# Norm output turned back on TensorE, gate row made in the attention phase, shared output in full-row buffers

## The chip, the cores and the metric

The kernel runs on one core of one Trainium2 chip. The metric is the device time of one execution in microseconds (us). The kernel before takes 3271.61 us, the median of 3 runs (3268.63 to 3282.35). The engines are TensorE (PE, and PEld for its weight loads), VectorE (DVE), ScalarE (ACT), GpSimd (POOL) and SyncE (SP, which only issues DMAs here).

## What is computed

512 tokens of width 1024 go through one block of a first network and two layers of a second one, all in float32. Only the middle of the first block matters here. With `c` the conditioning vector, six rows of width 1024 come from it, among them `g1, sh2, sc2, g2`:

```python
mod = (c_act @ w_ada[l] + b_ada[l])[:, None, :]
sh1, sc1, g1, sh2, sc2, g2 = jnp.split(mod, 6, axis=-1)
...
x = x + g1 * (jnp.concatenate([o_hg, o_nsa], axis=-1) @ w_out[l])
h = rmsnorm(x, norm2_g[l]) * (1.0 + sc2) + sh2
x = x + g2 * moe_ffn(h, router_w[l], router_bias[l], w_exp_gu[l], w_exp_dn[l], w_sh_gu[l], w_sh_dn[l])
```

`moe_ffn` scores 64 experts for every token (a sigmoid of `h @ router_w`), takes the best 8 of the best 4 groups of 8, and adds to the weighted output of those experts the output of one shared expert that sees all tokens. Every expert is a gated product of hidden width 256.

## The kernel before

The program runs in phases: a (first norm and its first projections), b (two mixers, attention and the output projection), c (experts) and d (the second network). Matrix products of float32 data are made of three passes over a split of both operands into a rounded high part and a rest: `mm3` (L158 to L162) issues the passes, and `split` (L164 to L167) makes the parts, the high one by a cast on ACT and the rest by a subtraction on DVE.

**The order of the work.** The text of the program is not the order on an engine. A planner places the instructions of each engine by a model of their times (the kernel is built with `schedule_with_timeline_sim=True`), and `after` (L154) pins a few of them behind others. Each engine then works through its own list in order, so an instruction that waits holds back all behind it. POOL's list holds its DMA issues too, SP's those of the weights.

**Rows of the conditioning.** `b_mods` (L395) is a generator. `tick` advances it between pieces of the attention, so that the big products `c_act @ w_ada` are done a few rows at a time beside it: `mod_acc` (L180) multiplies on DVE and adds on POOL into a tile of 128 partial rows. From that, `mod_cols` (L200, matmuls on L205) makes the sum as 8 columns of 128, and `row_bc` (L897, matmuls on L903, sums on L904) makes it as a full row that stands in all 128 partitions. `g2` is made as columns only, `g1` as a row only, `sh2` and `sc2` (here `B2` and `A2`) in both forms. These rows live in the three `macc` buffers.

**The norm before the experts.** The output projection at the end of phase_b runs in two halves `h` of 256 tokens, and each half ends in a norm: sums of squares on ACT (L593), one scaling on DVE to `h2` (L597), then for each pair `k` of 128-column pieces four transposes on PE (L604), a scale and shift into `t2` (ACT L611, DVE L613) and a split into `self.hh, self.hl`. That is the transposed norm, which the router and the shared expert read. The experts gather rows of tokens instead, so the same norm is made a second time in rows: POOL multiplies `h2` by `A2` (L622), adds `B2` (L623), and writes it to memory as `h2d` (L624).

**From the router to the first expert.** `router(1)` on PE gives the logits, ACT copies them (`lgT`, L618), and phase_c (L1019) transposes them, applies the sigmoid (L1058), and makes the choice of experts by a long row of small DVE instructions. Their end is a list of tokens for the first three experts (`iidx`, L1259), which `gather` (L1200, an indirect DMA of POOL's queue) uses to fetch rows of `h2d` into the `ring` tiles, which POOL has set to zero (L1043). Meanwhile the second half of the shared expert runs (`shared_up`, then `shared_down`, L1002). `shared_down` makes eight pieces of 128 tokens by 512 columns; each is multiplied by `g2` on DVE (L1016) into a tile `sy` with two buffers (tag `ey`) and written to `accd[1]` by POOL's queue (L1017). `g2` as a row is made here from its columns: POOL makes eight diagonal tiles (L1065), PE sums them (L1066), ACT copies the result (L1067).

For the experts after the first three, the kernel orders all 64 by their load: it transposes the choice and the weights, copies them to `sT` (L1144, also tag `ey`), permutes them (L1147), and loops over the experts. In PE's list these permutations stand just before and between the first expert's transposes (L1299).

**The loop over experts.** Expert n loads 3 MB of weights by SP's queue, gathers the rows of expert n + 4, and adds its output to `accd` by an indirect DMA.

Of the kernel before, what the change touches and what calls it, by code (L numbers as in the profile page):

```python
# [8 lines left out]
F32 = mybir.dt.float32  # L9
# [5 lines left out]
AF = mybir.ActivationFunctionType  # L15
OP = mybir.AluOpType
AX = mybir.AxisListType

S = 512
# [122 lines left out]
class Kern:  # L142
# [252 lines left out]
    def b_mods(self):  # L395

        yield from self.mod_sub(0, 0, pool=True)
        for v in self.mod_acc(self.p["w_ada"][0], self.cact, 5 * D, pool=True):
            if v is None:
                yield  # L400
        self.g2c = self.cp.tile([128, 8], F32, name="g2c")
        self.mod_cols(v, self.g2c, self.vec("b_ada", 40, 8), "sc")
        yield
        rows, cols = [], []
        for n in (2, 3, 4):
            for v in self.mod_acc(self.p["w_ada"][0], self.cact, n * D, pool=True):
                if v is None:
                    yield
            rows.append(v)
            if n > 2:  # L410
                t = self.cp.tile([128, 8], F32, name=f"mc{n}")
                self.mod_cols(v, t, self.vec("b_ada", n * 8, 8), "sc")
                cols.append(t)
            self.row_bc(v, n * D, "sc")
            yield
        self.g1, self.B2, self.A2 = rows
        self.B2c, self.A2c = cols
        self.nc.vector.scalar_tensor_tensor(self.A2c, self.A2c, 1.0, self.vec("norm2_g", 0, 8), op0=OP.add, op1=OP.mult)
        gb = self.m4.tile([128, D], F32, name="gb", tag="mraw", bufs=2)
        self.nc.gpsimd.dma_start(gb, self.p["norm2_g"][0:1, :].to_broadcast([128, D]))  # L420
        self.nc.vector.scalar_tensor_tensor(self.A2, self.A2, 1.0, gb, op0=OP.add, op1=OP.mult)
        yield

    def kv_proj(self, win):
# [54 lines left out]
    def phase_b(self):  # L479
# [82 lines left out]
        def router(h):  # L562
            hs = slice(h * 256, (h + 1) * 256)
            for k in range(KT):
                self.mm3(psr[0:64, hs], rwh[:, k], rwl[:, k], self.hh[:, k, hs], self.hl[:, k, hs], k == 0, k == KT - 1)

        for h in range(2):
# [31 lines left out]
            for k in range(0, KT, 2):  # L599
                ps = self.bank("tr")  # L600
                for kk in range(2):
                    for ii in range(2):
                        c0 = (2 * kk + ii) * 128
                        nc.tensor.transpose(ps[:, c0:c0 + 128], h2[:, ii, (k + kk) * 128:(k + kk + 1) * 128], self.ident)  # L604
                t2 = mid.tile([128, 512], F32, name="h2t", tag=("kraw", "pct")[k // 2 % 2], bufs=1)
                for kk in range(2):
                    t = t2[:, kk * 256:(kk + 1) * 256]
                    a, b = self.A2c[:, k + kk:k + kk + 1], self.B2c[:, k + kk:k + kk + 1]
                    pv = ps[:, kk * 256:(kk + 1) * 256]
                    if kk:  # L610
                        nc.scalar.activation(t, pv, AF.Identity, bias=b, scale=a)  # L611
                    else:
                        nc.vector.tensor_scalar(t, pv, a, b, op0=OP.mult, op1=OP.add)  # L613
                    self.split(t, self.hh[:, k + kk, hs], self.hl[:, k + kk, hs])
            if h:
                router(1)
                self.lgT = self.m4.tile([128, S], F32, name="lgT", tag="mraw", bufs=2)[0:64]
                nc.scalar.copy(self.lgT, psr[0:64, :])  # L618

            for ii in range(2):  # L620
                i = 2 * h + ii
                nc.gpsimd.tensor_tensor(h2[:, ii], h2[:, ii], self.A2, OP.mult)  # L622
                nc.gpsimd.tensor_tensor(h2[:, ii], h2[:, ii], self.B2, OP.add)  # L623
                nc.gpsimd.dma_start(self.h2d[i * 128:(i + 1) * 128, :], h2[:, ii])  # L624
        self.dump("x1", self.x1[:])

# [375 lines left out]
    def shared_down(self):  # L1002

        nc, c = self.nc, self.cpool
        for i in range(4):
            nc.gpsimd.dma_start(self.accd[0][i * 128:(i + 1) * 128, :], self.x1[:, i])
        for half in range(2):
            cs = slice(half * 512, (half + 1) * 512)
            dh, dl = self.dn_piece(self.shd, half)
            for i in range(4):  # L1010
                ahl = self.sha[i // 2]
                ps = self.bank("dn")
                for k in range(2):
                    self.mm3(ps, ahl[:, 0, i % 2, k], ahl[:, 1, i % 2, k], dh[:, k], dl[:, k], k == 0, k == 1)
                y = c.tile([128, 512], F32, name="sy", tag="ey", bufs=2)
                nc.vector.tensor_tensor(y, ps, self.g2[:, cs], OP.mult)  # L1016
                nc.gpsimd.dma_start(self.accd[1][i * 128:(i + 1) * 128, cs], y)  # L1017

    def phase_c(self):  # L1019
        nc, p, c = self.nc, self.p, self.cpool  # L1020
# [19 lines left out]
        self.ring = []  # L1040
        for n in range(4):
            r = c.tile([128, D], F32, name=f"ring{n}", tag="ring", bufs=4)
            nc.gpsimd.memset(r, 0.0)  # L1043
            self.ring.append(r)

        psl = self.bank("tr")
# [9 lines left out]

        sco = t4("sco")
        sig = nc.scalar.activation(f(sco), psl[:, 0:256], AF.Sigmoid)  # L1058

        self.g2 = self.m4.tile([128, D], F32, name="g2", tag="macc", bufs=3)  # L1060
        for a in range(2):
            ps = self.bank("at")
            for j in range(4):
                dg = c.tile([128, 128], F32, name="dg", tag="dg", bufs=2)
                nc.gpsimd.tensor_tensor(dg, self.ident, self.g2c[:, 4 * a + j:4 * a + j + 1].to_broadcast([128, 128]), OP.mult)  # L1065
                nc.tensor.matmul(ps[:, j * 128:(j + 1) * 128], self.ones, dg, start=True, stop=True)  # L1066
            nc.scalar.copy(self.g2[:, a * 512:(a + 1) * 512], ps)  # L1067
        cho = t4("cho")
        nc.vector.tensor_tensor(cho, sco, bias[:, None, :].to_broadcast(E4), OP.add)
        t8 = c.tile([128, 32, 8], F32, name="t8", tag="es", bufs=2)  # L1070
# [68 lines left out]
        for src in (sel, wt):  # L1139
            pst = self.bank("tr")  # L1140
            for i in range(4):
                nc.tensor.transpose(pst[0:NE, i * 128:(i + 1) * 128], src[:, i], self.ident)
            sT = c.tile([NE, S], F32, name="sT", tag="ey", bufs=2)
            nc.scalar.copy(sT, pst[0:NE, :])  # L1144
            pso = self.bank("dn")
            for i in range(4):
                nc.tensor.matmul(pso[:, i * 64:(i + 1) * 64], sT[:, i * 128:(i + 1) * 128], perm, start=True, stop=True)  # L1147
            nc.vector.tensor_copy(f(src), pso[:, 0:256])
# [696 lines left out]
def body(tc, p, dbg=None, stop=None):  # L1845
    K = Kern(tc, p, dbg, stop)
    PS = bass.MemoryType.PSUM
    with tc.tile_pool(name="cst", bufs=1) as K.cp, \
# [26 lines left out]


_INS = ["x", "w_ada", "b_ada", "w_in", "hg_norm_g", "cmp_w1_k", "cmp_w2_k", "cmp_w1_v", "cmp_w2_v", "w_out",
        "norm2_g", "router_w", "router_bias", "w_exp_gu", "w_exp_dn", "w_sh_gu", "w_sh_dn", "w_mod_2",
        "w_ffn1_gu_2", "w_ffn1_down_2", "w_ffn2_gu_2", "w_ffn2_down_2", "w_in_2", "w_out_2", "attn_sinks_2",
        "lru_gate_a_w_2", "lru_gate_x_w_2", "final_g"]  # L1880

# [25 lines left out]
```

## Time and profile before

| what | before |
|---|---|
| median of 3 runs | 3271.61 us |
| the profiled execution | 3271.81 us |
| its span, first to last instruction | 3270.0 us |
| PE busy | 3091.5 us, 95% |
| DVE busy | 1929.4 us, 59% |
| ACT busy | 1232.5 us, 38% |
| POOL busy | 542.8 us, 17% |

The profile shows one execution. The busy time of an engine over the whole span is an average over stages: what a change is worth is read from the stage that it touches, from what each engine waits for there. Stage marks: attention to 442 us, output projection and second norm to 530 us, choice of experts and shared expert to 592 us, loop over experts to about 1313 us, then phase d.

### The profile page before, as it was taken

How to read it: one execution, taken by the hardware profiler on the slowest of the kernel's cores; microseconds unless marked ns; L12 is line 12 of the kernel's file. 1: busy time of each engine (PE TensorE's matmuls, PEld its weight loads, DVE VectorE, ACT ScalarE, POOL GpSimd, SP SyncE). 2: the span in 40 equal slices, each digit the busy share in tenths (PEclk: the TensorE clock that was granted, in tenths of full speed). 3: DMA queues.
4: the chain of work that ended last, by engine and by line, in shares of the span. 5: the costliest groups of instructions: out<-in, count | busy, mean ns of one | idle time of the engine just before them, and what ended most of it. 6: DMA issues, size and time to landing. Idle time of an engine off the chain costs nothing.

```text
span 3270.0 us, 40750 instructions
## 1 busy us (share of the span) xinstructions
PE 3091.5 (95%) x15632; PEld 2356.4 (72%) x15633; DVE 1929.4 (59%) x2962; ACT 1232.5 (38%) x1976; POOL 542.8 (17%) x374
## 2 busy tenths in 40 slices
PE   6998997899999997799999999999999999999999
PEld 5876575555555554677888697888877888788888
DVE  6776767777767766665347665334664356653335
ACT  5133453444444544422235442223422245442223
POOL 0255515222233323100011110000000010100001
PEclk9998998899999999899999999999999999999999
DMA  6554335699899997675234255223664333233223
GB/s 242 163 164 155 110 127 193 226 347 340 306 318 338 336 331 240 208 228 176 89 119 116 70 173 195 90 91 110 202 217 155 99 127 91 71 116 101 92 90 104
DMA packets 317928, 577.64 MB, mean 177 GB/s; under 512 B 49584, under 2 KB 252144, under 8 KB 293152
## 3 DMA queue, kind: packets, MB, share of 16 engines
q1 hardware_dynamic: 294000, 527.27, 47.3%
q0 software_dynamic: 21648, 45.60, 5.7%
q8 instruction: 125, 2.05, 0.3%
q10 hardware_dynamic: 2080, 2.10, 0.2%
q14 instruction: 75, 0.61, 0.1%
HBM read 551.89 MB, written 28.39 MB: 177 GB/s over the span
## 4 chain that ended last, share of the span: by engine, by line
PE 71%; DMA 12%; DVE 9%; issue 4%; POOL 2%; ACT 2%; SPq 0%; DVEq 0%; POOLq 0%; ACTq 0%
PE ps_fm L162 9%; PE ps_fm L160 9%; PE ps_fm L161 9%; DMA mraw<-in_w_mod_dram 7%; PE ps_dn L1329 5%; PE ps_dn L160 5%; PE ps_dn L162 5%; PE ps_dn L161 5%; PE ps_gu L160 3%; PE ps_gu L161 3%; PE ps_gu L162 3%; DVE macc L195 2%; PE ps_tr L1299 2%; DMA wraw<-in_w_exp_gu_dram 2%; DVE wlo L167 1%
## 5 line engine op out<-in xcount | busy, mean ns | idle before, releaser
L167 DVE TENSOR_TENSOR wlo<-wraw,whi 128x1024 fp32r<-128x1024 f32 x480 | 575.6, 1204 | 568.7 <-ACT whi L166 560.7
L166 ACT CAST whi<-wraw 128x1024 fp32r<-128x1024 f32 x480 | 487.3, 1017 | 875.2 <-PE ps_fm L161 371.4
L160 PE MATMUL ps_fm<-dhh,whi 128*128 128x512 f32 (+1 forms) x1808 | 677.1, 377 | 18.1 <-ACT whi L166 7.1
L162 PE MATMUL ps_fm<-dhh,wlo 128*128 128x512 f32 (+1 forms) x1808 | 667.8, 378 | 15.9 <-DVE wlo L167 15.8
L161 PE MATMUL ps_fm<-dhl,whi 128*128 128x512 f32 (+1 forms) x1808 | 675.8, 375 | 1.1 <-DVE dhl L1515 0.4
L162 PEld LDWEIGHTS ps_fm<-dhh,wlo 128*128 128x128 f32 x1808 | 341.7, 190 | 80.8 <-DVE wlo L167 20.2
L160 PEld LDWEIGHTS ps_fm<-dhh,whi 128*128 128x128 f32 x1808 | 340.8, 190 | 81.9 <-ACT whi L166 9.2
L161 PEld LDWEIGHTS ps_fm<-dhl,whi 128*128 128x128 f32 x1808 | 342.1, 189 | 63.1 <-DVE dhl L1515 2.8
L160 PE MATMUL ps_dn<-ah,whi 128*128 128x256 f32 (+1 forms) x1152 | 383.8, 335 | 1.5 <-DVE xT L1590 1.4
L161 PE MATMUL ps_dn<-al,whi 128*128 128x256 f32 (+1 forms) x1152 | 382.4, 332 | 0.0
L162 PE MATMUL ps_dn<-ah,wlo 128*128 128x256 f32 (+1 forms) x1152 | 382.4, 334 | 0.0
L167 DVE TENSOR_TENSOR wlo<-wbig,whi 128x1024 fp32r<-128x1024 f32 x192 | 231.8, 1219 | 98.4 <-ACT whi L166 98.1
L166 ACT CAST whi<-wbig 128x1024 fp32r<-128x1024 f32 x192 | 198.9, 1047 | 97.8 <-PE ps_gu L162 77.3
L160 PEld LDWEIGHTS ps_dn<-ah,whi 128*128 128x128 f32 x1152 | 216.8, 188 | 24.9 <-DVE xT L1590 2.5
L161 PEld LDWEIGHTS ps_dn<-al,whi 128*128 128x128 f32 x1152 | 216.7, 188 | 25.1 <-issue 1.5
L162 PEld LDWEIGHTS ps_dn<-ah,wlo 128*128 128x128 f32 x1152 | 216.1, 188 | 23.9 <-issue 0.8
L161 PE MATMUL ps_gu<-wlo,th 128*128 128x512 f32 (+21 forms) x512 | 210.4, 411 | 11.2 <-DVE wlo L167 11.2
L1477 POOL TENSOR_TENSOR sq<-sq 128x256 f32<-128x256 f32 x72 | 77.8, 1080 | 855.5 <-issue 720.1
L160 PE MATMUL ps_gu<-whi,th 128*128 128x512 f32 (+21 forms) x512 | 211.5, 413 | 3.7 <-ACT whi L166 3.6
L162 PE MATMUL ps_gu<-whi,tl 128*128 128x512 f32 (+21 forms) x512 | 203.5, 397 | 0.0
L195 DVE SCALAR_TENSOR_TENSOR macc<-mraw,cact,macc 128x1024 f32<-128x1024 f32 x105 | 134.7, 1282 | 107.0 <-DMA mraw<-in_w_mod_dram 106.5
L1590 DVE SCALAR_TENSOR_TENSOR xT<-ps_dn,modc,xT 128x256 f32<-128x256 f32 (+1 forms) x160 | 93.3, 587 | 157.8 <-PE ps_dn L162 156.4
(532 smaller groups left out, 4389.4 us busy)
## 6 DMA issues: line engine op xcount, KB each, us to landing
wbig<-in_w_exp_gu_dram SPq DMA_DIRECT2D x96, 1024.0 KB, 13.9
wraw<-in_w_ffn_gu_dram SPq DMA_DIRECT2D x86, 1024.0 KB, 5.1
mraw<-in_w_mod_dram SPq DMA_DIRECT2D x144, 512.0 KB, 4.3
dnraw<-in_w_exp_dn_dram SPq DMA_DIRECT2D x48, 1024.0 KB, 10.0
wraw<-in_w_exp_gu_dram SPq DMA_DIRECT2D x32, 1024.0 KB, 13.3
wraw<-in_w_ffn_down_dram SPq DMA_DIRECT2D x32, 1024.0 KB, 5.0
wraw<-in_w_out_dram SPq DMA_DIRECT2D x24, 1024.0 KB, 5.0
wraw<-in_w_ffn_down_dram SPq DMA_DIRECT2D x32, 768.0 KB, 4.3
```

Source lines behind the costliest of these rows:

```text
L160: mm(ps, ah, bh, start=first, stop=False)
L161: mm(ps, ah, bl, start=False, stop=False)
L162: return mm(ps, al, bh, start=False, stop=last)
L166: self.copied = self.nc.scalar.copy(hi, src)
L167: self.nc.vector.tensor_tensor(lo, src, hi.bitcast(F32), OP.subtract)
L195: nc.vector.scalar_tensor_tensor(acc, w, cact[:, k:k + 1], acc, op0=OP.mult, op1=OP.add)
L1299: nc.tensor.transpose(ps[:, k * 128:k * 128 + m], g[0:m, 4 * a + k:D:8], self.ident[0:m, 0:m])
L1329: self.mark2 = nc.tensor.matmul(ps[0:m], af[:, k, 0:m], dv[:, k, cs], start=k == 0, stop=k == 1)
L1477: nc.gpsimd.tensor_tensor(self.ssq, self.ssq, t, OP.add)
L1590: nc.vector.scalar_tensor_tensor(self.xT[:, k, hs], ps[j], G[:, k:k + 1], self.xT[:, k, hs], op0=OP.mult, op1=OP.add)
```

## The change

`b_mods` makes `g2` as a row (in a `macc` buffer that stays taken) and `sh2`, `sc2` as columns only; the load of `norm2_g` as a row goes. The rows of the norm for the experts are no longer computed a second time: the finished transposed tile `t2` is turned back by four transposes on PE into a bank `pb`, and ACT copies that into `h2`. The sigmoid is called once on a single column (`sgw`) ahead of the last router pass. POOL no longer makes the diagonals for `g2`, and the zeros of the ring move to DVE. The shared output gets four buffers of full rows (two of tag `ey`, two of `macc`) and four DMAs instead of eight, and `sT` moves from tag `ey` to tag `tl`.

```diff
@@ b_mods
-        for v in self.mod_acc(self.p["w_ada"][0], self.cact, 5 * D, pool=True):
-            if v is None:
-                yield
-        self.g2c = self.cp.tile([128, 8], F32, name="g2c")
-        self.mod_cols(v, self.g2c, self.vec("b_ada", 40, 8), "sc")
-        yield
-        rows, cols = [], []
-        for n in (2, 3, 4):
+        cols, rows = [], []
+        for n in (3, 4, 2, 5):
             for v in self.mod_acc(self.p["w_ada"][0], self.cact, n * D, pool=True):
                 if v is None:
                     yield
-            rows.append(v)
-            if n > 2:
+            if n in (3, 4):
                 t = self.cp.tile([128, 8], F32, name=f"mc{n}")
                 self.mod_cols(v, t, self.vec("b_ada", n * 8, 8), "sc")
                 cols.append(t)
-            self.row_bc(v, n * D, "sc")
+            else:
+                self.row_bc(v, n * D, "sc")
+                rows.append(v)
             yield
-        self.g1, self.B2, self.A2 = rows
+        self.g1, self.g2 = rows
...
-        gb = self.m4.tile([128, D], F32, name="gb", tag="mraw", bufs=2)
-        self.nc.gpsimd.dma_start(gb, self.p["norm2_g"][0:1, :].to_broadcast([128, D]))
-        self.nc.vector.scalar_tensor_tensor(self.A2, self.A2, 1.0, gb, op0=OP.add, op1=OP.mult)
@@ phase_b, inside the loop over pairs k
+                pb = self.bank("pj" if h else "sc")
+                for ii in range(2):
+                    for kk in range(2):
+                        c0 = (2 * ii + kk) * 128
+                        nc.tensor.transpose(pb[:, c0:c0 + 128], t2[:, kk * 256 + ii * 128:kk * 256 + ii * 128 + 128],
+                                            self.ident)
+                nc.scalar.copy(h2[:, :, k * 128:(k + 2) * 128], pb[:].rearrange("p (i c) -> p i c", i=2))
             if h:
+
+                sgw = bp.tile([128, 1], F32, name="sgw")
+                nc.scalar.activation(sgw, self.eps, AF.Sigmoid)
                 router(1)
...
             for ii in range(2):
                 i = 2 * h + ii
-                nc.gpsimd.tensor_tensor(h2[:, ii], h2[:, ii], self.A2, OP.mult)
-                nc.gpsimd.tensor_tensor(h2[:, ii], h2[:, ii], self.B2, OP.add)
                 nc.gpsimd.dma_start(self.h2d[i * 128:(i + 1) * 128, :], h2[:, ii])
@@ shared_down
+        ys = [self.m4.tile([128, D], F32, name="sy", tag="macc", bufs=3) if i % 2 else
+              c.tile([128, D], F32, name="sy", tag="ey", bufs=2) for i in range(4)]
...
-                y = c.tile([128, 512], F32, name="sy", tag="ey", bufs=2)
-                nc.vector.tensor_tensor(y, ps, self.g2[:, cs], OP.mult)
-                nc.gpsimd.dma_start(self.accd[1][i * 128:(i + 1) * 128, cs], y)
+                nc.vector.tensor_tensor(ys[i][:, cs], ps, self.g2[:, cs], OP.mult)
+                if half:
+                    nc.gpsimd.dma_start(self.accd[1][i * 128:(i + 1) * 128, :], ys[i])
@@ phase_c
-            nc.gpsimd.memset(r, 0.0)
+            nc.vector.memset(r, 0.0)
...
-        self.g2 = self.m4.tile([128, D], F32, name="g2", tag="macc", bufs=3)
-        for a in range(2):
-            ps = self.bank("at")
-            for j in range(4):
-                dg = c.tile([128, 128], F32, name="dg", tag="dg", bufs=2)
-                nc.gpsimd.tensor_tensor(dg, self.ident, self.g2c[:, 4 * a + j:4 * a + j + 1].to_broadcast([128, 128]), OP.mult)
-                nc.tensor.matmul(ps[:, j * 128:(j + 1) * 128], self.ones, dg, start=True, stop=True)
-            nc.scalar.copy(self.g2[:, a * 512:(a + 1) * 512], ps)
...
-            sT = c.tile([NE, S], F32, name="sT", tag="ey", bufs=2)
+            sT = c.tile([NE, S], F32, name="sT", tag="tl", bufs=2)
```

The name `norm2_g` also leaves the list of inputs `_INS`.

## Rows read from the trace of the kernel before

**Rows 1.** Windows of 10 us: PE, PEld, DVE, ACT, POOL busy, then PEclk, DMA share, GB/s.
```profile
520.00:530.00 10.00, 3.13 (x12) 1.87 (x12) 10.00 (x8) 1.91 (x6) 10.00 (x7) 0.76 0.02 6
...
560.00:570.00 10.00, 6.25 (x23) 4.48 (x22) 4.12 (x18) 0.00 (x0) 4.31 (x5) 0.52 0.57 185
...
580.00:590.00 10.00, 5.05 (x22) 4.08 (x21) 3.39 (x6) 2.79 (x4) 1.08 (x2) 0.66 0.25 97
```

**Rows 2.** Timeline of POOL, 430 to 660 us: start, length, then what ran.
```profile
489.78 5.45 POOL L622 TENSOR_TENSOR h<-h,macc 128x1024 f32<-128x1024 f32 x2 [15.94 <-PE ps_tr L604]
...
518.30 5.48 POOL L622 TENSOR_TENSOR h<-h,macc 128x1024 f32<-128x1024 f32 x2 [13.14 <-PE ps_tr L604]
...
529.82 3.65 POOL L1043 MEMSET ring<- 128x1024 f32 x4
...
561.48 1.10 POOL L1200 DMA_INDIRECT ring<-h2d,iidx  x1 [8.86 <-DVE iidx L1259]
```

**Rows 3.** Timeline of DVE, 480 to 660 us.
```profile
485.34 0.42 DVE L167 TENSOR_TENSOR h2l<-h2t,h2h 128x256 fp32r<-128x256 f32 x1
...
490.35 2.62 DVE L167 TENSOR_TENSOR h2l<-h2t,h2h 128x256 fp32r<-128x256 f32 x1
...
520.21 8.83 DVE L167 TENSOR_TENSOR h2l<-h2t,h2h 128x256 fp32r<-128x256 f32 x4
...
529.11 4.45 DVE L1033 TENSOR_SCALAR tri<-cpk 128x128 bf16<-128x128 f32 x1
...
539.98 1.23 DVE L954 TENSOR_TENSOR wlo<-wraw,whi 128x1024 fp32r<-128x1024 f32 x1 [1.52 <-ACT whi L953]
...
564.36 1.27 DVE L1016 TENSOR_TENSOR sy<-ps_dn,g 128x512 f32<-128x512 f32 x2
```

**Rows 4.** Waits of PE, 480 to 660 us: total us, times, longest.
```profile
PE ps_dn L160 <- DVE sy L1016: 8.8, 3, 6.4
...
PE ps_sc L161 <- DVE h2l L167: 7.2, 4, 4.4
...
PE ps_dn L1147 <- ACT sT L1144: 4.9, 1, 4.9
...
PE ps_sc L160 <- ACT h2h L166: 2.3, 2, 1.7
...
PE ps_sc L161 <- DVE wlo L167: 1.9, 1, 1.9
```

**Rows 5.** Waits of DVE, 480 to 660 us.
```profile
DVE sy L1016 <- DMA acc1d<-sy: 15.0, 3, 10.2
```

**Rows 6.** Timeline of ACT, 470 to 640 us.
```profile
529.87 0.58 ACT L618 COPY lgT<-ps_sc 64x512 f32<-64x512 f32 x1 [8.09 <-issue]
...
531.25 1.28 ACT L1058 ACT_TABLE_LOAD   x1 [0.81 <-PE ps_tr L1048]
...
585.40 0.58 ACT L1144 COPY sT<-ps_tr 64x512 f32<-64x512 f32 x1 [3.23 <-DMA acc1d<-sy]
```

**Rows 7.** Timeline of PE, 553 to 600 us.
```profile
592.34 0.78 PE L160 MATMUL ps_gu<-whi,th 128*128 128x512 f32 x1
```

**Rows 8.** Chain that ended last, 400 to 720 us: start, length, what.
```profile
412.08 1.68 PE ps_sc L205 x16
...
413.76 0.97 PE ps_sc L903 x2
...
482.65 0.66 PE ps_tr L604 x6
```

**Rows 9.** Source lines: landing of the gathers (tile ring), a memset of L222.
```profile
DMA to landing us min/median/max: 4.2/12.1/17.8
...
L222 DVE MEMSET ones<- x1: 165/165/165, 0.9 to 0.9; 128x128 f32 x1
```

**Rows 10.** Windows in the expert loop, columns as in rows 1.
```profile
620.00:1080.00 460.00, 456.22 (x1967) 236.81 (x1965) 339.03 (x692) 223.46 (x340) 128.35 (x85) 0.99 0.95 330
...
1220.00:1240.00 20.00, 17.74 (x76) 10.98 (x75) 12.45 (x16) 10.66 (x16) 6.27 (x3) 1.00 0.96 316
```

More of the change, by code (lines that the diff above doesn't have):

```diff
@@ L1877 @@
 _INS = ["x", "w_ada", "b_ada", "w_in", "hg_norm_g", "cmp_w1_k", "cmp_w2_k", "cmp_w1_v", "cmp_w2_v", "w_out",
-        "norm2_g", "router_w", "router_bias", "w_exp_gu", "w_exp_dn", "w_sh_gu", "w_sh_dn", "w_mod_2",
+        "router_w", "router_bias", "w_exp_gu", "w_exp_dn", "w_sh_gu", "w_sh_dn", "w_mod_2",
         "w_ffn1_gu_2", "w_ffn1_down_2", "w_ffn2_gu_2", "w_ffn2_down_2", "w_in_2", "w_out_2", "attn_sinks_2",
```

## The prediction

> **What bounds the kernel now.** I read the windows first, because the change touches only the stretch from the attention to the first expert, and PE's 95% over the whole span hides what that stretch looks like. PE is busy 3.13 of 10 us from 520 to 530, 6.25 from 560 to 570 and 5.05 from 580 to 590, and its granted clock falls to 0.76, 0.52 and 0.66 of full speed there, against 456.22 of 460 at clock 0.99 in the first part of the expert loop [rows 1, 10]. So before the loop PE is not the bound. Two stalls are to be seen.
>
> The first is at 490 and at 520 us. POOL multiplies and adds the rows of the norm, two tiles of rows in about 5.5 us for each of the two steps and each half [rows 2]. Beside it the same DVE subtraction that took 0.42 us at 485.34 takes 2.62 us, and four of them take 8.83 us [rows 3]. In 520 to 530 both engines count as busy all the time [rows 1], so DVE is not working but held by POOL. PE then waits 7.2 us for the rests of the norm, 2.3 us for its high parts and 1.9 us for a weight rest, 11.4 us in all [rows 4].
>
> The second lies after the first gather, issued at 561.48 [rows 2]. DVE waits 15.0 us, once for 10.2, for the writes of `sy` to leave its two buffers [rows 5]; PE waits 8.8 us for DVE at the same place and 4.9 us for `sT`, which has the same two buffers and is held until 585.40 [rows 4, 6]. The first expert's matmuls start at 592.34 [rows 7], 30.9 us after the gather was issued. A gather lands in 4.2 us at best and 12.1 in the median [rows 9], so its data is not what is late.
>
> **The change, part by part.** The sum is made against the profiled execution, 3271.81 us (span 3270.0), which is 0.2 us from the median of the runs.
>
> *Rows in the attention phase.* One column sum (1.68 us of PE) and one row (two such pieces of 0.97 us, so 1.9 us) fall away [rows 8], with their sums on DVE and one load of a row; the load of `norm2_g` goes as well. Both stand in the chain that ended last, so up to 3.6 us; nothing if PE only waits a little longer for a softmax. I take 3, as the chain ran through them.
>
> *Norm.* All eight long POOL operations go, and with them the 11.4 us of waiting. Added are 32 transposes on PE at 0.66/6 = 0.11 us, 3.5 us in all [rows 8], in a place where PE has work, and eight copies on ACT; the nearest row is the copy of 64x512 at 0.58 us [rows 6]. Six of them I cost at nothing, as ACT was busy only 1.91 of 10 us in 520 to 530 [rows 1]; two can stand in front of the copy of the logits, 1.2 us. If that cover is gone all eight cost 4.6 us. Net -11.4 + 3.5 + 1.2 = -6.7; ends -10 (the transposes fill holes) and -2 (all copies in line, and some waits stay because ACT is late next). The write of `h2d` moves from behind POOL's addition to behind the last copy; POOL has nothing else queued there, and the gather comes over 20 us later.
>
> *Sigmoid.* The table load of 1.28 us between logits and sigmoid [rows 6] is made ahead by `sgw`: -1.3. If the planner puts `sgw` ahead of the gate of the shared expert, two loads more: +2.6. The Trainium skill (ScalarE: Activation LUTs, What ACT_TABLE_LOAD costs) counts a drain of about 1.38 us on top of the load for each switch; no row here shows that drain, and by it the sum would be 1.4 us better.
>
> *Zeros of the ring.* POOL's four take 3.65 us [rows 2], and `tri` on DVE took 4.45 us beside them [rows 3], in a hole in which DVE waits for the logits anyway. On DVE a memset of 128 columns takes 0.165 us [rows 9], so 1024 columns at most 1.32, four 5.3 us; about 3.65 if DVE is as fast as POOL. The hole is shorter by the table load: +1, ends 0 and +5.3. The Trainium skill (SBUF — State Buffer, Who interferes with whom) says that a GpSimd instruction that only writes does not hold a DVE instruction with two inputs, only one of the two-port kind. The trace agrees as far as `tri` goes. By that rule POOL's zeros held up nothing but two small casts, DVE loses the full 3.65, and the sum is 2.7 us worse.
>
> *Choice of experts.* The diagonals and the two copies for `g2` go, which were beside the chain. DVE stood three times behind ACT and PE here, at most 1.52 us each [rows 3], since PE ran at a clock below 1 after its hole; at most 4.6 us come back. Against it, six of the eight multiplications by `g2`, two in 1.27 us [rows 3], stood behind the gather and may now stand ahead of it: +3.8. I take 0.
>
> Up to the gather: -3 - 6.7 - 1.3 + 1 + 0 = -10, so the gather goes at about 551.5.
>
> *From the gather to the first expert.* With four buffers no multiplication waits for a landing, and `sT` waits for no write. PE's 8.8 + 4.9 = 13.7 us are the least that goes. If the shared expert is done by then, what is left is the landing of the gather and PE's work from `sT` at 585.40 to 592.34, some 7 us, of which a part overlaps: about 8.5, or -22.4. With a landing of 12.1 and the last 4 us of that work it is 30.9 - 16.1 = -14.8. I take -18: the landing was short when the queues were empty, but some of the shared expert's passes will still be in front. What is late next is the gather itself.
>
> Sum: -10 - 18 = -28, so 3271.8 - 28 = 3243.8. I cost what follows at nothing: the loop and phase d keep their lists, and the loads for the first experts are issued by SP as the shared expert frees buffers, so they move up with it.
>
> **The rivals.**
>
> *The gathers queue behind the row writes.* POOL's list holds both, and a row write now needs both halves of the shared expert. For it: in the list of before, writes stand between gathers and choice. If all four stand ahead of the gather, it goes when the shared expert is through, at about 558, and the first expert starts 12.1 + 4.3 later at 574.4: -18, 3254.
>
> *PE stands at the turned-back transposes.* Each set needs `t2`, which ACT and DVE have just made. If the planner puts them straight behind, PE waits about 1 us at eight places: 8 us given back, 3252. For it: PE's list is in order; against it: the planner has other matmuls there.
>
> *The loop gives the gain back.* DMA is at a share of 0.95 already where PE is busy 456 of 460 [rows 10]. If weights set the end of the loop, an earlier start is worth only what DMA idled before it (share 0.25 in 580 to 590 [rows 1]). Half of the gain then stays: 3258, no change that can be told.
>
> *The loop runs short of weights (slower).* If the loop starts before the loads have their lead, PE may wait for weights as in 1220 to 1240, where it is busy 17.74 of 20 [rows 10]. At that pace the 460 us from 620 to 1080 [rows 10], where PE loses next to nothing, would take 20/17.74 as long, 58 us more: 3272 - 28 + 58 = 3302. It decides from half of that stretch on (29 us lost). Against it: DMA idles just before the loop, so the lead is there.
>
> **How the numbers follow.** A measurement here can tell 0.5%, 16.4 us, from no change. The forecast gets 0.55, the queue of POOL 0.13, PE standing 0.12, the gain given back 0.14, the slower one 0.06. The forecast's own range is 3230 (all good ends: -3.6 - 10 - 1.3 - 4.6 - 22.4 = -42) to 3256. The range to hold it 8 times in 10 takes in the second to fourth cases: 3230 to 3262. Faster by over 0.5% (under 3255.3): the forecast without its worst tail 0.53, PE standing 0.12, POOL's queue 0.09, together 0.74; slower 0.06; the same 0.20.
>
> **What would show it.** Right: no DVE subtraction over 1 us in the norm; the logits' copy (529.87 before [rows 6]) at about 520; sigmoid without a table load in front; no DVE wait for a landing of `sy`; the first expert's matmuls at about 564, and the loop's end as much earlier. Wrong: PE waits for `t2`, DVE's zeros in front of the first sum of the choice, gathers issued behind row writes, or PE under 19 of 20 in the loop's first half.

## The result, and the profile after

The changed kernel takes 3237.47 us in the median of 5 runs (3228.99 to 3243.84); the kernel before 3268.63 us, also in 5 runs (3260.02 to 3282.35). The ratio is 0.990 with an interval of 0.9869 to 0.9932. The forecast was 3243.8 us, with a range of 3230 to 3262; the gain is 31.2 us in the medians, 34.5 us between the two profiled spans (3270.0 and 3235.5), against 28 forecast.

Of the 34.5 us, 31 stand between the end of the attention and the first expert, and 3.9 in the loop. The marks below are starts of single instructions in the timelines: the first transpose behind the attention (L547, after: L539), the copy of the logits, the first sum of the choice (`cho`), the first gather, the first matmul on `whi` and `th`, the first transpose of the final stage. The last column is the step that the prediction made.

| step, us | before | after | difference | forecast |
|---|---|---|---|---|
| start to end of attention | 441.6 | 442.7 | +1.1 | -3 |
| norm, to the copy of the logits | 88.3 | 77.6 | -10.7 | -6.7 |
| logits to first sum of the choice | 3.7 | 4.0 | +0.4 | -0.3 (sigmoid and zeros) |
| choice, to the first gather | 27.9 | 30.5 | +2.5 | 0 |
| gather to first expert's matmul | 30.9 | 7.6 | -23.2 | -18 |
| loop over experts | 728.4 | 724.5 | -3.9 | 0 |
| from there to the end | 1949.3 | 1948.6 | -0.7 | 0 |

So the sum was near, but only by terms that miss in both directions. First the windows of the changed kernel (window, its length, busy of PE, PEld, DVE, ACT and POOL, then PEclk, DMA share, GB/s):

```profile
520.00:530.00 10.00, 9.33 (x44) 7.55 (x43) 7.04 (x19) 4.56 (x6) 4.25 (x8) 1.00 0.49 173
550.00:560.00 10.00, 6.75 (x40) 5.32 (x38) 5.73 (x31) 0.58 (x1) 3.12 (x3) 0.50 0.50 175
560.00:570.00 10.00, 10.00 (x58) 8.33 (x57) 9.62 (x27) 5.42 (x8) 0.00 (x0) 0.84 0.83 321
...
580.00:590.00 10.00, 10.00 (x44) 6.35 (x43) 8.61 (x17) 4.98 (x7) 5.99 (x4) 1.00 0.83 293
```

Where PE was busy 3.13, 6.25 and 5.05 of 10 us [rows 1] it is now busy 9.33, 10.00 and 10.00, though the later windows hold later work than before, since the first expert comes 30 us earlier. The hole left is in the choice, up to 560. Next DVE, by lines, 480 to 520 us (busy us, mean ns; then idle before), and its timeline around the logits and the list of rows (start, length, what, idle before):

```profile
L167 DVE TENSOR_TENSOR h2l<-h2t,h2h 128x256 fp32r<-128x256 f32 x16 | 6.5, 419 | 1.1 <-ACT h2h L166 1.0
```

```profile
519.76 0.16 DVE L1035 TENSOR_SCALAR tri<-cpk 128x128 bf16<-128x128 f32 x1
...
520.21 0.91 DVE L1045 MEMSET ring<- 128x1024 f32 x1 [0.16 <-issue]
...
523.43 0.91 DVE L1045 MEMSET ring<- 128x1024 f32 x1 [0.16 <-issue]
524.27 0.36 DVE L1062 TENSOR_TENSOR cho<-sco,cpk 128x256 f32<-128x256 f32 x1
...
545.92 0.68 DVE L1017 TENSOR_TENSOR sy<-ps_dn,macc 128x512 f32<-128x512 f32 x1
...
554.31 0.16 DVE L1252 TENSOR_TENSOR iidx<-slt,slu 128x3 int32<-128x3 f32 x1
```

The sixteen subtractions take 419 ns each in the mean, where they took up to 2.62 us beside POOL's norm [rows 3]. The four zeros (0.91 us, 0.16 idle before each) stand directly ahead of the first sum of the choice, and the eighth multiplication by `g2` ahead of `iidx`, on which the gather waits. ACT, POOL and PE at the same places:

```profile
519.29 0.59 ACT L614 COPY h<-ps_pj 128x512 f32<-128x512 f32 x1
520.24 0.58 ACT L621 COPY lgT<-ps_sc 64x512 f32<-64x512 f32 x1 [0.36 <-PE ps_sc L162]
520.84 1.28 ACT L1060 ACT_TABLE_LOAD   x1
522.13 0.38 ACT L1060 ACTIVATE sco<-ps_tr 128x256 f32<-128x256 f32 x1
...
547.52 0.58 ACT L1137 COPY sT<-ps_tr 64x512 f32<-64x512 f32 x1 [0.68 <-PE ps_tr L1135]
```

```profile
542.95 0.53 POOL L1019 DMA_DIRECT2D acc1d<-sy  x1 [18.53 <-DVE sy L1017]
...
546.90 0.53 POOL L1019 DMA_DIRECT2D acc1d<-sy  x1 [0.84 <-DVE sel L1092]
554.76 1.10 POOL L1193 DMA_INDIRECT ring<-h2d,iidx  x1 [7.33 <-DVE iidx L1252]
```

```profile
562.40 0.78 PE L160 MATMUL ps_gu<-whi,th 128*128 128x512 f32 x1
```

The copy of the logits comes at 520.24 (529.87 before [rows 6]), `sT` at 547.52 (585.40), the first expert at 562.40 (592.34 [rows 7]). But the table load of 1.28 us still stands ahead of the sigmoid. The view of `sgw`'s line tells why: the made-ahead sigmoid reads only `eps`, and the planner put it at the very start, over 500 us ahead, with other table loads in between.

```profile
L618 ACT ACT_TABLE_LOAD  x1: 1283/1283/1283, 0.8 to 0.8; - x1
L618 ACT ACTIVATE sgw<-eps x1: 203/203/203, 2.1 to 2.1; 128x1 f32<-128x1 f32 x1
```

What PE waits for, 480 to 660 us (total us, times, longest), has shrunk from waits of 8.8, 7.2 and 4.9 us [rows 4] to this, and DVE's wait for the landing of `sy` (15.0 us [rows 5]) is gone:

```profile
PE ps_dn L1140 <- DVE perm L1130: 1.2, 1, 1.2
PE ps_tr L1135 <- DVE sel L1092: 1.1, 1, 1.1
```

### The profile page after: what moved, and what is told of

Read it like the earlier page. It is cut to its first block, busy times and chain, and to the rows that moved or that the text cites. A ratio compares the mean times of both kernels' runs of the same rounds, so it can differ in the third digit from the quotient of the medians.

```text
span 3235.5 us, 40712 instructions
## 1 busy us (share of the span) xinstructions
PE 3081.7 (95%) x15628; PEld 2347.8 (73%) x15629; DVE 1910.3 (59%) x2962; ACT 1237.5 (38%) x1984; POOL 507.8 (16%) x348
## 4 chain that ended last, share of the span: by engine, by line
PE 74%; DMA 12%; DVE 8%; issue 3%; ACT 2%; POOL 1%; SPq 0%; DVEq 0%; POOLq 0%; ACTq 0%
PE ps_fm L162 9%; PE ps_fm L161 9%; PE ps_fm L160 9%; DMA mraw<-in_w_mod_dram 8%; PE ps_dn L1322 6%; PE ps_dn L160 5%; PE ps_dn L162 5%; PE ps_dn L161 5%; PE ps_gu L160 3%; PE ps_gu L161 3%; PE ps_gu L162 3%; DVE macc L195 2%; PE ps_tr L1292 2%; PE ps_pj L161 1%; DMA wraw<-in_w_exp_gu_dram 1%
## 5 line engine op out<-in xcount | busy, mean ns | idle before, releaser
L160 PE MATMUL ps_fm<-dhh,whi 128*128 128x512 f32 (+1 forms) x1808 | 676.3, 376 | 19.7 <-ACT whi L166 11.6
L162 PE MATMUL ps_fm<-dhh,wlo 128*128 128x512 f32 (+1 forms) x1808 | 666.6, 377 | 15.4 <-DVE wlo L167 15.3
L160 PEld LDWEIGHTS ps_fm<-dhh,whi 128*128 128x128 f32 x1808 | 340.2, 189 | 83.6 <-ACT whi L166 13.7
L1470 POOL TENSOR_TENSOR sq<-sq 128x256 f32<-128x256 f32 x72 | 77.6, 1078 | 856.7 <-issue 721.4
```

Of the source, the lines that this page charges most:

```text
L160: mm(ps, ah, bh, start=first, stop=False)
L162: return mm(ps, al, bh, start=False, stop=last)
L1470: nc.gpsimd.tensor_tensor(self.ssq, self.ssq, t, OP.add)
```

## The experiments

Twelve kernels, each read at the same marks. "Stages" means the seven steps of the table above. The kernel before, in the runs that accompany these, had medians of 3264 to 3266 us; its profiled execution, on which the stages stand, took 3271.81.

**e1_old_sy**: the changed kernel with the shared output as before: two half-row buffers, eight half-row writes, `sT` in the same two buffers.

```diff
-        ys = [self.m4.tile([128, D], F32, name="sy", tag="macc", bufs=3) if i % 2 else
-              c.tile([128, D], F32, name="sy", tag="ey", bufs=2) for i in range(4)]
...
-                nc.vector.tensor_tensor(ys[i][:, cs], ps, self.g2[:, cs], OP.mult)
-                if half:
-                    nc.gpsimd.dma_start(self.accd[1][i * 128:(i + 1) * 128, :], ys[i])
+                y = c.tile([128, 512], F32, name="sy", tag="ey", bufs=2)
+                nc.vector.tensor_tensor(y, ps, self.g2[:, cs], OP.mult)
+                nc.gpsimd.dma_start(self.accd[1][i * 128:(i + 1) * 128, cs], y)
...
-            sT = c.tile([NE, S], F32, name="sT", tag="tl", bufs=2)
+            sT = c.tile([NE, S], F32, name="sT", tag="ey", bufs=2)
```

> The changed kernel, with the shared output back in two half-row buffers, eight writes, and sT back behind them. Theory (the stall is the landing of these writes): the logits' copy stays at about 520 us and the gather at about 551 to 555, but DVE waits 10 to 15 us for landings again and the first expert's matmuls come 25 to 31 us after the gather instead of 7.6; time about 15 to 23 us over the changed kernel, near 3255. Rival (the wait came from g2 being late and from the split list of the choice, not from the buffers): since g2 is early here, no wait for a landing over 3 us, first expert 8 to 12 us after the gather, time within 5 us of the changed kernel, 3237 to 3242.

Measured: 3257.48 us, ratio 0.998 (0.9965 to 0.9996). Norm 77.6, gather to first expert 24.4 us, just under the 25 to 31 expected. From the attention's end to the loop's end it gains 19.0 us on the kernel before, the whole change 34.9: 15.9 us hang on this part. But it is not DVE that stands. The waits of 540 to 580 us:

```profile
PE ps_dn L1138 <- ACT sT L1135: 12.1, 1, 12.1
ACT sT L1135 <- DMA acc1d<-sy: 12.0, 2, 10.7
...
DVE sy L1016 <- DMA acc1d<-sy: 1.0, 1, 1.0
```

PE stands for `sT`, and `sT` for the writes that leave the buffers it shares. Two edits were in one; e9 and e10 part them.

**e2_new_sy**: the kernel before with the four full-row buffers and `sT` out of them, nothing else (the reverse of e1's diff).

> The kernel before, with nothing changed but the four full-row buffers, four writes, and sT in the other buffer. Theory (each part stands alone): logits' copy at 530 as before, gather 2 to 4 us later than before because all eight multiplications by g2 stand ahead of it in DVE's list, 564 to 566; first expert 8 to 10 us after the gather, 573 to 575; about 18 us under the kernel before, 3251. Rival (the buffers only help when the norm is out of the way): first expert still over 20 us after the gather, gain under 8 us.

Measured: 3252.67 us, ratio 0.9957 (0.9937 to 0.9978). Gather to first expert 7.6 us instead of 30.9, but the choice takes 32.9 instead of 27.9: all eight multiplications by `g2` now stand ahead of `iidx` (549.66 to 561.03, `iidx` at 565.09), where the kernel before had its second pair at 564.36 [rows 3], behind the gather. Norm stays at 88.1. The first expert, 592.34 before:

```profile
573.16 0.79 PE L160 MATMUL ps_gu<-whi,th 128*128 128x512 f32 x1
```

**e3_norm**: the kernel before with the norm's rows made by the turned-back transposes instead of POOL's two operations; rows, zeros, sigmoid and shared output stay.

```diff
+                pb = self.bank("pj" if h else "sc")
...
+                nc.scalar.copy(h2[:, :, k * 128:(k + 2) * 128], pb[:].rearrange("p (i c) -> p i c", i=2))
...
-                nc.gpsimd.tensor_tensor(h2[:, ii], h2[:, ii], self.A2, OP.mult)
-                nc.gpsimd.tensor_tensor(h2[:, ii], h2[:, ii], self.B2, OP.add)
```

> The kernel before, with nothing changed but the rows of the norm turned back on PE and copied by ACT instead of made on POOL; the rows A2 and B2 are still made but not used. Theory (DVE was held by POOL): no subtraction of 256 columns over 0.5 us, logits' copy about 10 us earlier, at 519 to 521, gather about 551, but the wait for landings of the shared output remains, so the first expert comes at 578 to 583; gain about 10 us, 3259. Rival (the second stall sets the first expert's start whatever comes before it): logits' copy 10 us earlier, first expert still at 588 to 592, no gain, 3267 to 3270.

Measured: 3250.51 us, ratio 0.9966 (0.9949 to 0.9983). Norm 76.6 us, gather to first expert 31.6. The subtractions of the norm by lines, 470 to 512 us, and the first expert:

```profile
L167 DVE TENSOR_TENSOR h2l<-h2t,h2h 128x256 fp32r<-128x256 f32 x16 | 6.5, 420 | 1.0 <-ACT h2h L166 1.0
```

```profile
570.42 0.78 PE L160 MATMUL ps_gu<-whi,th 128*128 128x512 f32 x1
```

In the stages the two gains are separate and nearly add: from the attention's end to the loop's end e2 gains 17.4 us and e1, which is the change without that part, 19.0, together 36.4 against 34.9; e3 gains 10.9 of e1's 19.0. Of the rest, 6.5 us lie between gather and first expert (24.4 in e1, 30.9 before, 31.6 in e3); which other part of the change gives them, the early `g2` being one candidate, no run parts. In the medians of whole runs the parts gain 6.8 (e1), 11.6 (e2) and 13.7 us (e3), so these show no such sum: they take in the attention and all that follows.

The attention ended 8.4 us earlier than before, though up to its end the trace has the same instructions in the same order on every engine as the kernel before. So does e2, which ended it at 440.9. Executions of one list can differ there by as much; the table below e11 shows that it is the clock.

**e4_pool_zero**: the changed kernel with the zeros of the ring on POOL.

```diff
-            nc.vector.memset(r, 0.0)
+            nc.gpsimd.memset(r, 0.0)
```

> The changed kernel, with the four zero fills of the ring back on POOL. Theory (on DVE they stand in front of the first sum of the choice): that sum starts 1.5 to 2 us earlier after the logits' copy, at +2.3 us instead of +4.0, and the gather as much earlier; 2 us under the changed kernel, not to be told in the time. Rival (POOL's zeros hold the two small casts on DVE, which stand ahead of the sum): the casts take 3.5 to 4.5 us each again and the sum starts at +3.6 or later, no gain.

Measured: 3236.2 us, ratio 0.9919 (0.9902 to 0.9936), no difference from the changed kernel. The first sum of the choice follows the logits by 2.3 us instead of 4.0, so DVE's zeros do cost 1.7 us there. On POOL they take as long as before, and hold nobody: `tri` is already through, and the first sum, which ran beside them, took 0.42 us. A subtraction that stands beside a later POOL operation takes 3.20 us, where such a one took 1.23 us [rows 3]:

```profile
516.65 0.16 DVE L1035 TENSOR_SCALAR tri<-cpk 128x128 bf16<-128x128 f32 x1
...
519.44 0.42 DVE L1062 TENSOR_TENSOR cho<-sco,cpk 128x256 f32<-128x256 f32 x1 [2.50 <-ACT sco L1060]
...
522.30 3.20 DVE L167 TENSOR_TENSOR wlo<-wraw,whi 128x1024 fp32r<-128x1024 f32 x1
```

```profile
518.10 3.65 POOL L1045 MEMSET ring<- 128x1024 f32 x4
521.68 3.19 POOL L1217 CAST RH<-cpk 128x12 bf16<-128x12 f32 x6
```

**e5_sgw_pin**: the changed kernel with `sgw` made to follow the Silu of the shared expert.

```diff
-            nc.scalar.activation(s, pss[ii][:, 0:256], AF.Silu)
+            self.gate = nc.scalar.activation(s, pss[ii][:, 0:256], AF.Silu)
...
+                with self.after(self.gate):
                     nc.scalar.activation(sgw, self.eps, AF.Sigmoid)
```

> The changed kernel with the dummy sigmoid pinned behind the shared expert's Silu on ScalarE. Theory: the 1.28 us table load disappears between the copy of the logits and the sigmoid of the scores, and the scores come about 1.3 us earlier, but the choice's first sum still stands behind four zeros of 0.91 us on VectorE, so it starts only 0 to 0.5 us earlier (4.1 us after the copy of the logits, now 3.6 to 4.1); time 3237, no difference that can be told. Rival: the first sum comes 1.3 us earlier, because the zeros had run into the wait for the table load; 2.8 us after the copy of the logits. Second rival: two table loads are added around the shared expert, and the copy of the logits comes 1 to 2.6 us later.

Measured: 3239.25 us in one run. The load between logits and sigmoid is gone, and stands 7 us earlier, in line with the norm's copies, and the logits come 2.1 us later (norm 79.7). The second rival held in its delay; no load was added, one moved:

```profile
511.25 1.28 ACT L995 ACT_TABLE_LOAD   x1
...
513.98 1.28 ACT L619 ACT_TABLE_LOAD   x1
515.27 0.20 ACT L619 ACTIVATE sgw<-eps 128x1 f32<-128x1 f32 x1
...
522.50 0.58 ACT L622 COPY lgT<-ps_sc 64x512 f32<-64x512 f32 x1
```

**e6_late_sy**: the changed kernel with the second half's four multiplications by `g2` behind the list of rows.

```diff
+        self.listed = nc.vector.tensor_tensor(iidx, t[:, :, 2], u, OP.add)
...
+                with self.after(self.listed if half else None):
                     nc.vector.tensor_tensor(ys[i][:, cs], ps, self.g2[:, cs], OP.mult)
```

> The changed kernel with the four second-half multiplications by g2 pinned behind the list of rows on VectorE, so that they and the four row writes no longer stand ahead of the gathers. Theory (after the choice was lengthened by 2.5 us because VectorE does eight multiplications ahead of the gather): gather at 552.1 instead of 554.8 (choice 28 instead of 30.5 us), but the first expert needs its rows, sT and the shared expert's end, so it starts 0 to 2.7 us earlier, 559.7 to 562.4; time 3234.8 to 3237.5. Rival A (the row writes in front of the gathers cost the time, as one of the rivals had it): gather earlier by over 4 us, gather to first expert unchanged at 7.6, so time under 3233.5. Rival B (the multiplications only move into the hole behind the gather and hold the banks of PE): first expert later by 1 us or more, time 3238.5 or above.

Measured: 3239.87 us, ratio 0.9929 (0.991 to 0.9948). Choice 27.4 us instead of 30.5, as expected; but gather to first expert takes 8.5, and the loop, in which PE now waits 2.1 us for the gather to land, 728.9 instead of 724.5 us. In its first 80 us PE is busy 75.9 us; in the changed kernel 79.5. The multiplications are the whole of the 2.5 us of the choice, and taking them out of it gains nothing: the rest of the shared expert is then done inside the loop.

**e7_mods**, and later **e11_mods**: the changed kernel with the same four rows of the conditioning made in another order beside the attention: (2, 5, 3, 4) in e7, and in e11 (5, 2, 3, 4), the order of before.

```diff
-        for n in (3, 4, 2, 5):
+        for n in (2, 5, 3, 4):
```

> The changed kernel with the rows made in the order 2, 5, 3, 4 instead of 3, 4, 2, 5; the same work. Theory (the attention phase gave nothing because TensorE, busy without a gap from about 340 us on, ran at half clock from 352 to 379 us, which hangs on the order of its work and not on its amount): the stretch moves or goes, and the attention ends at 432 to 440 instead of 442.7, the time falls by as much, to 3227 to 3235. Rival (the attention's end is set by softmax and VectorE, so the rows taken away were never on its path): attention ends at 441 to 444 whatever the clock does, time 3236 to 3239.

> The changed kernel with the rows made in the order 5, 2, 3, 4, the order of before; the same work as the changed kernel. Theory (order decides how long TensorE runs at half clock in the attention phase, amount does not): busy time weighted with the granted clock from 140 us to the attention's end stays at 253 to 254 us as in all kernels with the shorter work, the time lost to half clock comes out unlike both 32 us (3, 4, 2, 5) and 54 us (2, 5, 3, 4), and the end of the attention moves by the difference; with before's 24 us lost, end at 434, time 3229. Rival (the half clock follows from the shorter work itself): lost 31 to 35 us, end at 441 to 444, time 3236 to 3239.

Measured: 3261.59 us, ratio 0.9987 (0.9972 to 1.0001), and 3260.42 us, 0.9987 (0.9974 to 1.0). The attention ends at 466.8 and 468.0 us instead of 442.7: the order alone takes back all but 4 to 5 us of the change's gain, and what is left is not told from nothing. From there to the end both take what the changed kernel takes (2796.2 and 2791.5, changed 2792.8). Windows, columns as above, of the changed kernel and then of e11:

```profile
340.00:360.00 20.00, 20.00 (x105) 12.22 (x106) 14.83 (x26) 11.93 (x25) 9.95 (x6) 0.79 0.40 132
360.00:380.00 20.00, 20.00 (x58) 8.49 (x56) 7.48 (x15) 6.52 (x18) 3.06 (x2) 0.53 0.19 53
380.00:400.00 20.00, 20.00 (x101) 9.37 (x100) 16.67 (x24) 9.79 (x27) 13.06 (x6) 1.00 0.36 106
```

```profile
360.00:380.00 20.00, 13.61 (x68) 7.47 (x67) 8.83 (x10) 5.13 (x11) 12.93 (x5) 0.78 0.35 111
380.00:400.00 20.00, 18.31 (x45) 8.74 (x46) 11.08 (x17) 4.91 (x15) 8.48 (x4) 0.50 0.39 120
400.00:420.00 20.00, 20.00 (x50) 8.01 (x50) 12.94 (x19) 6.66 (x17) 10.67 (x5) 0.50 0.17 52
420.00:440.00 20.00, 20.00 (x58) 9.54 (x57) 6.43 (x10) 5.53 (x14) 3.60 (x1) 0.50 0.00 1
440.00:460.00 20.00, 20.00 (x87) 8.35 (x87) 7.63 (x12) 9.66 (x22) 2.41 (x1) 0.84 0.00 0
```

PE is busy nearly without a gap and does less: the granted clock is 0.50, the lower of its two levels (1.2 GHz), for 27 us in the changed kernel and for 68 in e11. In the same kernel one score matmul takes 924 ns in 352 to 378 us and 535 ns in 380 to 440 (lines of PE, changed kernel; the second field behind the bar is the mean):

```profile
L875 PE MATMUL ps_sc<-kr,qr 64*128 64x384 f32 x16 | 13.2, 924 | 0.0
```

```profile
L875 PE MATMUL ps_sc<-kr,qr 64*128 64x384 f32 x16 | 7.3, 535 | 0.0
```

Cutting 140 us to the attention's end into windows of 2.5 us, with busy time multiplied by the granted clock as work, and the rest of the busy time as lost to the clock (PE's ends are modelled, so these sums are estimates):

| kernel, rows' order | from 140 us to the end | PE idle | work | lost to clock |
|---|---|---|---|---|
| before (5, 2, 3, 4) | 301.6 | 22.6 | 258.3 | 20.7 |
| e2_new_sy (as before) | 300.9 | 20.7 | 259.4 | 20.9 |
| e3_norm (as before) | 293.2 | 23.2 | 258.4 | 11.6 |
| after (3, 4, 2, 5) | 302.7 | 20.0 | 253.8 | 28.9 |
| e7_mods (2, 5, 3, 4) | 326.8 | 23.8 | 252.7 | 50.3 |
| e11_mods (5, 2, 3, 4) | 328.0 | 27.9 | 253.6 | 46.5 |

The rows that the change takes away are worth some 5 us of work (258.3 to 259.4 in three kernels with them, 252.7 to 254.2 in eleven without); what happens to the end of the attention is decided mostly by the clock. One list of instructions gives no one value: 11.6 to 20.9 us lost in the three kernels with the list of before, 28.8 to 34.2 in eight kernels with the order 3, 4, 2, 5, whose attention ends between 439.5 and 445.5 us (before, e2 and e3: 433.2 to 441.6). e7's theory had the right cause and the wrong sign; e11's had the work right (253 to 254 expected) and the end wrong by 34 us (its 24, 32 and 54 us lost count the clock in idle time too; by that count e11 lost 51). The order of before gives 20.7 in the kernel before and 46.5 in the changed one, so neither order nor amount alone foretells the clock.

**e8_best**: the edits of e4, e5 and e6 together.

> The changed kernel with three edits: zeros of the ring on GpSimd again, the dummy sigmoid pinned behind the shared expert's Silu, and the four late multiplications behind the list of rows. If the three pieces add (1.7 us of VectorE's zeros ahead of the choice, 1.3 us of table load, 0 to 2.7 us of the multiplications): logits copy to choice 1.3 us instead of 4.1, choice 28 instead of 30.5, first expert 3 to 5.5 us earlier on equal attention and norm, time about 3232 to 3234.5. Rival: each only moves a wait, because PE still has the shared expert to do before the first expert: time 3236 to 3238.

Measured: 3239.69 us, ratio 0.9917 (0.9903 to 0.9931). Logits to choice 1.5 us, choice 28.2, as the sum of the pieces; norm 79.6 (the moved table load) and a loop of 731.1 us take it back.

**e9_sT_ey** and **e10_two_sy** part the two edits of the shared output: e9 is the changed kernel with `sT` back in the buffers of the shared output, e10 the changed kernel with the two half-row buffers back, but `sT` kept out of them.

```diff
-            sT = c.tile([NE, S], F32, name="sT", tag="tl", bufs=2)
+            sT = c.tile([NE, S], F32, name="sT", tag="ey", bufs=2)
```

This is e9's diff; e10's is that of e1 without these two lines.

> The changed kernel with sT again in the two buffers that rows 0 and 2 of the shared output use; the four full-row buffers stay. Theory (what stood between gather and first expert was sT's wait for the row writes to land, and VectorE's own wait only second): TensorE stands for sT again, with the landing of the two writes as releaser, for 5 to 12 us; gather to first expert 13 to 20 us instead of 7.6, first expert at 568 to 575, time 3243 to 3250. Rival (four full-row buffers took the wait away, as the prediction put it first): gather to first expert 7 to 10 us, time 3236 to 3240.

> The changed kernel with the two half-row buffers and eight half-row writes of before, but sT kept out of them. Theory (sT's wait is the larger part): VectorE waits for landings of sy again, by up to 10 us, but TensorE goes on with other work and waits for sT no more than 2 us; gather to first expert 7.6 to 12 us, time 3237 to 3242. Rival (VectorE's wait for the buffers holds the banks of TensorE and so the first expert): gather to first expert 16 to 24 us, time 3246 to 3255, with TensorE waiting for VectorE's sy 5 us or more.

Measured: e9 3233.61 us, ratio 0.991 (0.9893 to 0.9926), gather to first expert 7.6 us. e10 3243.33 us, ratio 0.9932 (0.9913 to 0.9951), gather to first expert 7.4 us. Either edit alone removes the stall that is 24.4 us with neither (e1). e9's rival held, and e10's theory. What is left of the wait, first e9, then e10, 540 to 580 us:

```profile
ACT sT L1137 <- DMA acc1d<-sy: 1.9, 1, 1.9
```

```profile
PE ps_dn L1138 <- DVE sy L1016: 2.3, 1, 2.3
...
DVE sy L1016 <- DMA acc1d<-sy: 1.1, 1, 1.1
```

They are not quite alike: in e10 the second half's multiplications stay behind the gather, as in e6, and the loop is 734.3 us long. From the attention's end to the loop's end it is 844.2 us with both edits, 844.8 with the full-row buffers alone, 850.7 with `sT`'s alone, 860.1 with neither.

**e12_mods_best**: the edits of e4 and e6 and a fourth order, (5, 3, 4, 2).

> The changed kernel with the order 5, 3, 4, 2, the zeros of the ring on GpSimd and the four late multiplications behind the list of rows: the candidate for a version that beats both. From the attention's end to the first expert the sum of the two single edits is 119.7 - 2.0 - 2.2 = 115.5 us. With the attention's end at 430 to 443 the time is 3220 to 3233. Rival (an order with as much half clock as 2, 5, 3, 4): attention's end at 460 or later, time 3250 to 3256, whatever the two edits give.

Measured: 3255.63 us, ratio 0.9982 (0.997 to 0.9993). Attention's end to first expert 115.7 us, as the sum (115.5); but the attention ends at 461.0, with 49.4 us lost to the clock: the rival. No version here beats the changed kernel by more than the intervals allow; e9 and e4 stand beside it.

## Why the prediction came out as it did

*Rows in the attention phase (forecast -3, measured +1.1).* This step did not come true. The size of the removed work was near (some 5 us, the bound was 3.6), and it is PE's work. What the step left out is that PE's clock in this stretch depends on how the work is strung together, as e7, e11 and e12 show: between these two traces 8.2 us more were lost to half clock. Since executions of one list lie up to 8.4 us apart at this mark, the 4 us between forecast and measurement can't be told from that spread. The row for it was to be had before, at a clock of 0.81 with 18.98 of 20 us busy:

```profile
340.00:360.00 20.00, 18.98 (x86) 11.20 (x84) 14.26 (x20) 10.94 (x22) 8.71 (x4) 0.81 0.31 101
```


*Norm (forecast -6.7, measured -10.7, just outside the ends of -10 and -2).* The mechanism held: PE's idle time in the stage falls from 13.9 to 2.5 us, which is the 11.4 of [rows 4], and its work grows by 3.5 us, the 3.5 of the transposes. Mis-sized were the two other terms: the copies on ACT (1.2 us) cost nothing, because the copy of the logits waits for PE with ACT idle 0.36 us, and the 2.8 us that PE lost to a lower clock behind its waits came back, unpriced.

*Sigmoid (forecast -1.3, measured 0).* Failed: the planner moved the made-ahead sigmoid to 2.1 us, and the load stayed. e5 shows that where it does work it only moves the load ahead of the logits, which then come 2.1 us later. No drain beside the load is to be seen on ACT: in the rows above the logits' copy ends at 520.82, the load runs from 520.84 to 522.12 and the sigmoid begins at 522.13. The drain of 1.38 us that the Trainium skill (ScalarE: Activation LUTs, What ACT_TABLE_LOAD costs) counts is not seen here.

*Zeros of the ring (forecast +1, e4 says +1.7).* Right in kind: they do stand ahead of the first sum, and the hole covers part of their 4 x 1.07 us. That `tri` lay in a hole was misread by a little: it ran from 529.11 to 533.56 [rows 3], and the first sum started at 533.54, behind it. The Trainium skill (SBUF — State Buffer, Who interferes with whom) would have a two-input DVE subtraction undisturbed by a POOL operation that only writes; the trace of e4 agrees: the first sum of the choice, with two inputs, took 0.42 us beside POOL's zeros, and the subtraction that took 3.20 us stood beside POOL's casts, which read.

*Choice of experts (forecast 0, measured +2.5, within -4.6 to +3.8).* The +3.8 side was right: all eight multiplications stand ahead of `iidx`, and e6, which takes four of them out, has 3.1 us less. The clock gave back nothing.

*Gather to first expert (forecast -18, measured -23.2, ends -22.4 and -13.7).* PE's idle time falls from 14.4 to 1.2 us, 13.2 against the 13.7 that the step called the least. The rest, by the same count of work some 10 us, is work of the shared expert that was done ahead of the gather (6.2 us less work in the step, 1.9 more in the choice and 1.9 more ahead of it) and 3.8 us of clock. The step gave two reasons, the four buffers and `sT`'s own place, as if each carried its part (8.8 and 4.9). e1, e9 and e10 show that in the changed kernel each alone removes the whole stall of this step: what [rows 4] splits between two waits is one line of writes, and either way out of it is enough, though with `sT`'s alone the loop is then 10 us longer.

*The rivals.* The gathers do stand behind the four row writes in POOL's list, as the first rival had it, but the last write was issued at 546.90 and POOL then waited 7.33 us for `iidx`: the order came, the cost did not. PE stood 0.4 us at the turned-back transposes, not 8. The loop gave nothing back (it is 3.9 us shorter, and the clock of its first 80 us 1.00 instead of 0.97), and ran no shorter of weights: 460 us of it hold 456.33 us of PE at clock 1.00 and a DMA share of 0.95, as before [rows 10].

```profile
595.00:1055.00 460.00, 456.33 (x1971) 237.11 (x1971) 340.89 (x687) 226.62 (x345) 129.94 (x84) 1.00 0.95 332
```

The number was right because the misses cancel: -9.2 from norm and gather beyond the forecast, -4.6 from the loop and what follows, +7.3 from attention, sigmoid, zeros and choice. That it was right was in part luck, and the whole coming out 6 us under the forecast is no proof of its terms.

## What to carry to other kernels

When two waits in a view end in the same row of transfers, cost them as one, and try each way out alone: here another buffer for one small tile gives 9.4 of the 15.3 us, up to the loop's end, that four full-row buffers give. A made-ahead instruction that reads only a constant can be planned anywhere; tie it to the instruction behind which it is meant to run, and ask what then stands behind it. And where PE is busy 20 of 20 us, read the clock column before calling the stretch bound by work: here the attention of e11 ended 35 us later than that of e3 (468.0 against 433.2) with 5 us less work.

## What was not expected of the hardware

TensorE ran at half clock for 27 us (changed kernel, 351.5 to 378.8 us) and for 68 us (e11, 378 to 446), busy nearly all the time (28 of the 28 us from 351 to 379, 66.2 of 68). The fall came once after 10 us of unbroken work (10.00 of 10 from 340 to 350, changed kernel) and once after a stretch with holes (13.61 of 20 from 360 to 380, e11); what ends such a stretch the runs don't show, and what sets it off stays open. It is no accident of one run: all eight traces with the order 3, 4, 2, 5 have a stretch of 24 to 27 us at half clock that begins between 351 and 357 us, and the three with the list of before have none over 14 us from 140 us to the attention's end. The five timed runs of the changed kernel had mean clocks of 0.974 (3243.84 us) to 0.982 (3228.99 us), in the order of their times, and the ten of e11 0.967 to 0.975.
